# The order of wide and narrow matmuls in the up products of a two-layer decoder

## The chip, the cores and the metric

The kernel runs on one core of a Trainium2 chip. The metric is the time of one execution on the device, in microseconds. The engines are called as in the profile: PE (TensorE, with PEld for its weight loads), DVE (VectorE), ACT (ScalarE), POOL (GpSimd) and SP (SyncE, which here issues the transfers).

## The reference

The input has 256 tokens of 2048 channels. A first layer mixes tokens by an RWKV-7 recurrence (32 heads of 64) and then runs a multilayer perceptron (MLP); a second one runs attention over a window of 128 tokens, with shared keys and values, and then an MLP of its own. All arrays are float32. The change lies in the two MLPs:

```python
D_FF = 4 * D_MODEL          # 8192

def squared_relu_mlp(xn, w_up, w_down):
    return jnp.square(jax.nn.relu(xn @ w_up)) @ w_down

h = h + squared_relu_mlp(rms_norm(h, mlp_norm[layer]), mlp_w_up[layer], mlp_w_down[layer])
```

## The kernel before

**Products in high and low parts.** PE multiplies in a rounded form of float32 (fp32r). To keep the precision, each operand is split into a high part, which is the rounded value, and a low part, which is the rest, and a product is the sum high x high + high x low + low x high. Inputs are kept as tiles of 128 channels with both parts side by side: `xt[kt]` is 128 x (2 x 256 tokens). Weights come from memory in tiles `raw` of 128 x 1024 and are split in pieces of 512 columns: ACT writes the high part `wh` (L146), DVE the low part `wl` (L147). Each of the two has three buffers, `raw` has four.

**Up products.** `gemm_c` makes 128 of the 8192 hidden channels for all 256 tokens. The weights are the stationary operand, the inputs move. One piece of weights holds four blocks of 128 x 128, for four input tiles. Per block there are two matmuls: one of 512 moving columns, high weights with both parts of the input (L168), and one of 256, low weights with the high part alone (L170). Both add into one bank of PSUM: the left half collects high x high and low x high, the right half high x low. A product has four pieces, an MLP 64 products, and there are two MLPs.

**What follows.** ACT copies the right half, DVE adds the left one, applies the gain and the ReLU, ACT squares, and ACT and POOL split the result into high and low parts again (L1056 to L1062). After 16 up products come the down products of these 2048 hidden channels (`gemm_t`, L182 to L184): there the inputs are stationary and the weights move, always 512 columns.

**What sets the order.** In the RWKV part PE's order is the one written in the code (`rwkv_in_order`); short dependent products stand between pieces of long ones (`product`, L345 and L347, written like `gemm_c`). The rest is placed by a scheduler that simulates the engines and takes what is ready; where the code says `manual_schedule` for PE, the written order is kept among the matmuls inside, and others can still be placed between them. `gemm_t` uses it for its blocks, `gemm_c` does not. Each engine then runs its own list in order.

**Names in the prediction's steps.** `x_m` are the MLP's transposed inputs and `ps_u`, `ps_d` the sums of up and down products. In the RWKV part `merges` fetches blocks of inverses from memory as `X` and `XT`, 64 partitions at a time (L845), and multiplies them (L858); `three` (L686) makes the gate product with three matmuls of 256 columns for each of two blocks.

Of the kernel before, what the change touches and what calls it, by code (L numbers as in the profile page):

```python
# [17 lines left out]
P = 128  # L18
T = 256
D = 2048  # L20
KT = D // P
# [6 lines left out]
NXA, NXB = 32, 16  # L28
# pieces of long products between the short ones, in microseconds of the tensor engine
F1 = (5.0, 0.7, 3.0, 2.5, 3.0)  # L30
# [63 lines left out]

# columns of a pair's key side: [R | A | (B, K) | k' | E | XT]
S1W = 7 * T + 4
# [9 lines left out]
class K:  # L106
# [18 lines left out]

    # [P, 512] working tiles of the RWKV part, by role
    def t2(self, tag, name):
# [8 lines left out]

    # raw weights as four (hi, lo) pieces of 512 columns
    def split(self, raw, q, name):
# [19 lines left out]

    # out[c, t] (two halves: high x parts, low x parts) = sum_k W[k, c] x[k, t]
    def gemm_c(self, src, xt, name):  # L160
        nc = self.nc
        raw = self.load(src.rearrange("p k c -> p (k c)"), name)
        ps = self.acc(f"ps_{name}")
        for q in range(4):
            wh, wl = self.split(raw, q, f"{name}_{q}")
            for j in range(4):
                kt = 4 * q + j
                nc.tensor.matmul(ps, wh[:, j * P:(j + 1) * P], xt[kt].rearrange("p a t -> p (a t)"),  # L168
                                 start=(kt == 0), stop=False, skip_group_check=True)
                nc.tensor.matmul(ps[:, :T], wl[:, j * P:(j + 1) * P], xt[kt][:, 0, :],  # L170
                                 start=False, stop=(kt == KT - 1), skip_group_check=True)
        return ps

    # out[t, n] for one chunk of 512 columns, two token halves
    def gemm_t(self, srcs, xt, name, evac):
        nc = self.nc
        pss = [self.acc(f"ps_{name}_{t}") for t in range(2)]
        nk = 4 * len(srcs)

        def part(t, kb, wh, wl):  # L180
            tt = slice(t * P, (t + 1) * P)
            nc.tensor.matmul(pss[t], xt[kb][:, 0, tt], wh, start=(kb == 0), stop=False)  # L182
            nc.tensor.matmul(pss[t], xt[kb][:, 1, tt], wh, start=False, stop=False)  # L183
            nc.tensor.matmul(pss[t], xt[kb][:, 0, tt], wl, start=False, stop=(kb == nk - 1))  # L184
        todo = []
        for g, src in enumerate(srcs):
            raw = self.load(src.rearrange("p k c -> p (k c)"), f"{name}_{g}")
            for q in range(4):
                kb = 4 * g + q
                todo.append((kb, *self.split(raw, q, f"{name}_{g}_{q}")))  # L190
                # the last two blocks go by token half, so that the first half is done early
                if kb != nk - 2:
                    with self.tc.manual_schedule(engines={mybir.EngineType.PE}):
                        for t in range(2):
                            for w in todo:
                                part(t, *w)
                    todo = []
        for t in range(2):
            evac(t, pss[t])

    # 1/sqrt(v) for small v [P, n], v > 0
    def rsqrt(self, v, n, name):
# [3 lines left out]

    # rstd [P, 2] over the channels of h[t][n]
    def rstd(self, h, name, vector=False):
# [18 lines left out]

    # [P, T] tile whose column t holds rstd of token t
    def rstd_row(self, rs, name):
# [9 lines left out]

    # (h * gain)^T as high and low parts, one list of KT tiles per gain  # L240
    def xT(self, h, gains, name, tags, banks=("ps",)):
# [65 lines left out]

    # ---------------------------------------------------------------- RWKV
    # The tensor engine runs in the order written here: short dependent products, with pieces of long
    # products between them (fill) to cover the way through the other engines and back.  # L310
    def rwkv_in_order(self, h):
        with self.tc.manual_schedule(engines={mybir.EngineType.PE}):
            return self.rwkv()

    # run queued pieces for about us microseconds of the tensor engine
    def fill(self, us):
# [36 lines left out]
    def rwkv(self):  # L353
        tc, nc, d = self.tc, self.nc, self.d
        with ExitStack() as es:
# [5 lines left out]

            # scratch in DRAM: per pair results of the key side; block images of the inverses
            self.sp = [dr.tile([2, P, S1W - T], F32, name=f"sp{c}") for c in range(NPAIR // 2)]
            self.za = [dr.tile([64, 32, 64], F32, name=f"za{i}") for i in range(2)]
            self.zx = [dr.tile([4, 32, 32, 64], F32, name=f"zx{i}") for i in range(2)]
            # derived per-channel vectors
            hv = self.cp.tile([P, 4 * KT], F32, name="hv")
# [11 lines left out]

            # ---- norm, transpose, shift  # L380
            x = self.load_h0
# [4 lines left out]
            for g in range(KT // 2):  # L386
# [6 lines left out]
                ps = self.ps(f"xT{g}", banks[g])  # L393
                for jj in range(2):
                    kt = 2 * g + jj
# [27 lines left out]
            first = []  # L423
# [83 lines left out]

            # ---- key side: two pairs to a step; merges of the inverses follow three steps later
            xr, xv = [None] * KT, [None] * KT
# [9 lines left out]
            side = self.key_low(0)  # L519
# [6 lines left out]
            for s in range(8):  # L526
# [26 lines left out]
                if s < 7:  # L553
                    side = self.key_low(2 * s + 2)
# [8 lines left out]

            # ---- value side: one pair to a step
            stream = deque([(0, 2), (1, 2)] + [(p, i) for p in range(2, NPAIR) for i in (0, 2)])
            zs = []
            h = [[None] * 4 for _ in range(2)]
# [78 lines left out]
            for n in range(2):  # L646
                for t in range(2):
                    evac_n(n)(t, wo[n][t])
            # the first layer's rows are transposed between the last products
            self.xt0 = [[]]  # L650
# [12 lines left out]

    # the first block of columns of the output product, as far as zs goes
    def out_part(self, w, n, zs, out, bank):
# [16 lines left out]

    # out += w^T x, both as (high, low)
    def three(self, out, w, x, start, stop):
        for i, (a, b) in enumerate(((0, 0), (0, 1), (1, 0))):
            self.nc.tensor.matmul(out, w[a], x[b], start=(start and i == 0), stop=(stop and i == 2))  # L686

    # sum of the two halves of a channel-major product
    def join(self, dst, ps, name):
# [7 lines left out]

    # key side of pairs p, p + 1: decay and rate
    def key_low(self, p):
# [8 lines left out]
        for j in J:  # L708
            q = p + j
# [5 lines left out]
            nc.scalar.activation(ta[:, j], ps[:, T:], AF.Tanh, bias=self.hv[:, 16 + q:17 + q], scale=0.5)  # L715
        # decay: sums within a chunk, before and through each token
        nc.vector.tensor_scalar(pd[:, :, :, 1:], pd[:, :, :, 1:], 1.0, None, ALU.add)
# [7 lines left out]

    # sums of squares by token and head
    def key_norm(self, p, k, side):
# [32 lines left out]

    # normalised keys (negated), and what the chunks take from them
    def key_mid(self, p, k, side):
# [20 lines left out]

    # products within the chunks, masked
    def key_high(self, p, V, ats):
# [17 lines left out]

    # (I - Mab)^-1 for the four pairs of a group: 16 x 16 diagonal blocks by substitution, one block to a
    # partition
    def substitute(self, g):
# [19 lines left out]

    # blocks of the inverses of pairs 2c, 2c + 1 merged to 32, then to 64; X^T is kept
    def merges(self, c, ats):
# [22 lines left out]

        # out[po, :, :, n] = L[k, :, :, m]^T R[k, :, :, n]
        def mm(nm, po, k, L, m, R, n):
# [35 lines left out]

    # value side of pair p, before the chunks: scores, values by token, bonus  # L890
    def prep(self, p, rv, st):
# [6 lines left out]
        nc.vector.tensor_tensor(R, self.c4(r), E[:, :, 1:], ALU.mult)  # L898
        # scores, transposed: rows (b s | k s) for head 0, (k s | b s) for head 1; columns (r t | a t)
        SC = [[None] * NCH for _ in range(2)]  # L900
# [12 lines left out]
        yield 1.75  # L913
        # by token: (b, k) of each chunk; values under room for S (SV) and for the state products (ST)
        kr = [H[1], H[0]]
# [32 lines left out]

    # chunk by chunk
    def chain(self, p, st, hop):  # L950
# [46 lines left out]

    # group norm, by token
    def post(self, p, yps, ob):
# [15 lines left out]

    # back to channels; affine, bonus, gate
    def post_pe(self, p, post, zs):
# [23 lines left out]

    # ---------------------------------------------------------------- MLP
    def mlp(self, h, layer, xtag, htag):
# [25 lines left out]

    # ---------------------------------------------------------------- attention  # L1070
    def attention(self, h):
        tc, nc, d = self.tc, self.nc, self.d
        with ExitStack() as es:
# [7 lines left out]
            rs = self.rstd(h, "a")  # L1081
            # rotary tables with the norm gains folded in: [t][c * g | swapped signs]
            tabs = {}
# [29 lines left out]

            # shared keys and values
            vs = [ap.tile([P, T], F32, name=f"v_{t}") for t in range(2)]
# [71 lines left out]

    # transposed probabilities of heads a, a + 1: [key, (block 0: own | block 1: previous, own) x q]
    def softmax(self, a2, qT, kT, a, bank):
# [90 lines left out]
```

## Time and profile before

| | us |
|---|---|
| median of three timed runs | 2432.09 |
| the three runs | 2429.99, 2432.09, 2434.12 |
| span of the profiled execution | 2429.5 |
| PE busy in that span | 2342.7 |
| L168, 2048 matmuls of 512 columns, busy | 723.9 |
| L170, 2048 matmuls of 256 columns, busy | 574.9 |

The span goes from the first to the last instruction of the program in one profiled execution; the page states no other time of that execution. It lies 2.6 us below the median and 0.5 us below the fastest run. Busy time counts overlapping matmuls of a group once, and their ends are modelled, so a group's mean duration is longer than the step from one start to the next. A line "A <- B" in a list of waits says that A stood idle until B was done.

The run falls into four parts: RWKV until about 732 us, the first MLP until 1449, attention until about 1714, and the second MLP to the end. In each MLP four runs of up products take turns with four runs of down products.

### The profile page before, as it was taken

To read this page: it belongs to the slowest core of one execution; us is meant where nothing else is said; L and a number is where in the kernel's file an instruction comes from. 1 tells how busy PE (TensorE), PEld (TensorE's weight loads), DVE (VectorE), ACT (ScalarE), POOL (GpSimd) and SP (SyncE) were. 2 spreads that over 40 slices of the span, in tenths; PEclk is the share of its full clock that TensorE was granted. 3 is DMA by queue.
4 is the path that set the end of the run, shared out by engine and by line. 5 is a ranking of instruction groups with operands and counts; after the bars stand their busy time and mean duration, and the time that the engine had idled before them with its cause. 6 is when DMAs were issued, how large, how long until landed. Compare 5 with 4: busy or idle time off the path is not lost.

```text
span 2429.5 us, 40469 instructions
## 1 busy us (share of the span) xinstructions
PE 2342.7 (96%) x14448; PEld 1925.8 (79%) x14448; DVE 1560.0 (64%) x3126; ACT 1284.5 (53%) x2563; POOL 487.0 (20%) x635
## 2 busy tenths in 40 slices
PE   5878799999999999999999999999999999999999
PEld 4666677777788888888888887777888888888887
DVE  7887667777666656556556666766655655665655
ACT  5545333333356546546546565765654554554654
POOL 3657322334301101101001001641110110110100
PEclk9998899999999999999999999999999999999999
DMA  4665644444465565665565555334565655556565
GB/s 139 204 194 163 175 146 142 141 140 137 146 195 181 188 196 184 190 192 189 191 191 186 187 182 185 111 112 156 183 190 192 190 190 192 187 188 196 184 199 174
DMA packets 149642, 425.64 MB, mean 175 GB/s; under 512 B 38848, under 2 KB 46784, under 8 KB 149440
## 3 DMA queue, kind: packets, MB, share of 16 engines
q1 hardware_dynamic: 148000, 420.62, 54.5%
q10 hardware_dynamic: 1440, 2.44, 0.3%
q8 instruction: 113, 1.85, 0.3%
q14 instruction: 89, 0.73, 0.1%
HBM read 403.05 MB, written 19.96 MB: 174 GB/s over the span
## 4 chain that ended last, share of the span: by engine, by line
PE 88%; DVE 4%; DMA 4%; issue 1%; SPq 1%; ACT 1%; POOL 1%; ACTq 0%; DVEq 0%; POOLq 0%
PE ps_u L168 20%; PE ps_u L170 10%; PE ps_d L184 9%; PE ps_d L183 9%; PE ps_d L182 9%; PE ps_v L345 3%; PE ps_r L345 3%; PE ps_wo L678 2%; PE ps_wo L680 2%; PE ps_wo L679 2%; PE ps_q L184 1%; PE ps_q L182 1%; PE ps_q L183 1%; PE ps_v L347 1%; PE ps_r L347 1%
## 5 line engine op out<-in xcount | busy, mean ns | idle before, releaser
L168 PE MATMUL ps_u<-x_m,wh_u 128*128 128x512 f32 x2048 | 723.9, 399 | 0.0
L170 PE MATMUL ps_u<-x_m,wl_u 128*128 128x256 f32 x2048 | 574.9, 281 | 0.0
L147 DVE TENSOR_TENSOR wl_d<-raw_d,wh_d 128x512 fp32r<-128x512 f32 x512 | 354.5, 693 | 292.8 <-ACT wh_d L146 274.6
L147 DVE TENSOR_TENSOR wl_u<-raw_u,wh_u 128x512 fp32r<-128x512 f32 x512 | 354.8, 693 | 267.7 <-ACT wh_u L146 261.3
L146 ACT ACTIVATE wh_d<-raw_d 128x512 fp32r<-128x512 f32 x512 | 323.7, 632 | 347.2 <-DVE wl_d L147 260.6
L168 PEld LDWEIGHTS ps_u<-x_m,wh_u 128*128 128x128 f32 x2048 | 384.6, 188 | 95.1
L146 ACT ACTIVATE wh_u<-raw_u 128x512 fp32r<-128x512 f32 x512 | 324.2, 633 | 256.1 <-PE ps_u L168 238.3
L184 PE MATMUL ps_d<-wl_d,h 128*128 128x512 f32 x1024 | 399.0, 390 | 1.6 <-DVE wl_d L147 1.6
L182 PE MATMUL ps_d<-wh_d,h 128*128 128x512 f32 x1024 | 398.8, 389 | 0.0
L183 PE MATMUL ps_d<-wh_d,h 128*128 128x512 f32 x1024 | 398.5, 389 | 0.0
L170 PEld LDWEIGHTS ps_u<-x_m,wl_u 128*128 128x128 f32 x2048 | 386.9, 189 | 0.6
L1062 POOL TENSOR_TENSOR h<-w,h 128x256 fp32r<-128x256 f32 x128 | 115.6, 904 | 1124.7 <-ACT h L1061 1096.0
L184 PEld LDWEIGHTS ps_d<-wl_d,h 128*128 128x128 f32 x1024 | 192.2, 188 | 42.1 <-DVE wl_d L147 2.3
L182 PEld LDWEIGHTS ps_d<-wh_d,h 128*128 128x128 f32 x1024 | 192.2, 188 | 39.8
L183 PEld LDWEIGHTS ps_d<-wh_d,h 128*128 128x128 f32 x1024 | 192.2, 188 | 39.7
L345 PE MATMUL ps_k<-lk,wh_k 128*128 128x512 f32 x256 | 98.9, 423 | 6.9 <-DVE lk L414 6.3
L345 PE MATMUL ps_v<-lv,wh_v 128*128 128x512 f32 x256 | 101.7, 426 | 0.0
L345 PE MATMUL ps_r<-lr,wh_r 128*128 128x512 f32 x256 | 101.7, 427 | 0.0
L146 ACT ACTIVATE wh_v<-raw_v 128x512 fp32r<-128x512 f32 x64 | 40.4, 631 | 97.7 <-PE ps_v L345 37.4
L146 ACT ACTIVATE wh_r<-raw_r 128x512 fp32r<-128x512 f32 x64 | 40.3, 630 | 79.9 <-PE ps_v L345 32.9
L347 PE MATMUL ps_k<-lk,wl_k 128*128 128x256 f32 x256 | 75.6, 295 | 5.6 <-DVE wl_k L147 5.5
L1219 POOL TENSOR_SCALAR s<-s,den 128x128 f32<-128x128 f32 x64 | 61.8, 981 | 77.3 <-DVE den L1215 30.5
(308 smaller groups left out, 3754.9 us busy)
## 6 DMA issues: line engine op xcount, KB each, us to landing
raw_u<-in_up SPq DMA_DIRECT2D x256, 512.0 KB
raw_d<-in_down SPq DMA_DIRECT2D x256, 512.0 KB
raw_k<-in_wrkv SPq DMA_DIRECT2D x32, 512.0 KB
raw_r<-in_wrkv SPq DMA_DIRECT2D x32, 512.0 KB
raw_v<-in_wrkv SPq DMA_DIRECT2D x32, 512.0 KB
raw_wout<-in_wout SPq DMA_DIRECT2D x32, 512.0 KB
raw_q<-in_wq SPq DMA_DIRECT2D x32, 512.0 KB
S1b<-sp SPq DMA_DIRECT2D x16, 770.0 KB
```

Source lines behind the costliest of these rows:

```text
L146: nc.scalar.activation(wh, src, AF.Copy)
L147: nc.vector.tensor_tensor(wl, src, wh.bitcast(F32), ALU.subtract)
L168: nc.tensor.matmul(ps, wh[:, j * P:(j + 1) * P], xt[kt].rearrange("p a t -> p (a t)"), start=(kt == 0), stop=False, skip_group_check=True)
L170: nc.tensor.matmul(ps[:, :T], wl[:, j * P:(j + 1) * P], xt[kt][:, 0, :], start=False, stop=(kt == KT - 1), skip_group_check=True)
L182: nc.tensor.matmul(pss[t], xt[kb][:, 0, tt], wh, start=(kb == 0), stop=False)
L183: nc.tensor.matmul(pss[t], xt[kb][:, 1, tt], wh, start=False, stop=False)
L184: nc.tensor.matmul(pss[t], xt[kb][:, 0, tt], wl, start=False, stop=(kb == nk - 1))
L345: nc.tensor.matmul(ps, wh[:, j * P:(j + 1) * P], xt[kt].rearrange("p a t -> p (a t)"), start=(kt == 0), stop=False, skip_group_check=True)
L347: nc.tensor.matmul(ps[:, :T], wl[:, j * P:(j + 1) * P], xt[kt][:, 0, :], start=False, stop=(kt == KT - 1), skip_group_check=True)
L678: nc.tensor.matmul(pss[t], zs[kb][:, 0, tt], wh, start=(kb == 0), stop=False)
L1062: nc.gpsimd.tensor_tensor(hx[:, 1, :], w, hx[:, 0, :].bitcast(F32), ALU.subtract)
L1219: nc.gpsimd.tensor_scalar(ss[i][:, sl[t]], ss[i][:, sl[t]], den[:, i, t:t + 1], None, ALU.mult)
```

## The change

In `gemm_c` the four matmuls of 512 columns of a piece are issued first, then the four of 256, and both loops stand under `manual_schedule`, so that PE keeps this order. Everything else in the file differs in comments only. The core of the diff:

```diff
     def gemm_c(self, src, xt, name):
         nc = self.nc
         raw = self.load(src.rearrange("p k c -> p (k c)"), name)
         ps = self.acc(f"ps_{name}")
         for q in range(4):
             wh, wl = self.split(raw, q, f"{name}_{q}")
-            for j in range(4):
-                kt = 4 * q + j
-                nc.tensor.matmul(ps, wh[:, j * P:(j + 1) * P], xt[kt].rearrange("p a t -> p (a t)"),
-                                 start=(kt == 0), stop=False, skip_group_check=True)
-                nc.tensor.matmul(ps[:, :T], wl[:, j * P:(j + 1) * P], xt[kt][:, 0, :],
-                                 start=False, stop=(kt == KT - 1), skip_group_check=True)
+            with self.tc.manual_schedule(engines={mybir.EngineType.PE}):
+                for j in range(4):
+                    kt = 4 * q + j
+                    nc.tensor.matmul(ps, wh[:, j * P:(j + 1) * P], xt[kt].rearrange("p a t -> p (a t)"),
+                                     start=(kt == 0), stop=False, skip_group_check=True)
+                for j in range(4):
+                    kt = 4 * q + j
+                    nc.tensor.matmul(ps[:, :T], wl[:, j * P:(j + 1) * P], xt[kt][:, 0, :],
+                                     start=False, stop=(kt == KT - 1), skip_group_check=True)
         return ps
```

The lines of `gemm_c` are L169 and L173 afterwards, and lines behind it move by three.

PE's list in the middle of the first run of up products (product 9, first piece), before. `wh` and `wl` are the parts of the weights, the last field is the shape of the result:

```order
L168 MATMUL ps_u_9_9516<-x_m_0_8504,wh_u_9_0_9517 128x512
L170 MATMUL ps_u_9_9516<-x_m_0_8504,wl_u_9_0_9518 128x256
L168 MATMUL ps_u_9_9516<-x_m_1_8507,wh_u_9_0_9517 128x512
L170 MATMUL ps_u_9_9516<-x_m_1_8507,wl_u_9_0_9518 128x256
L168 MATMUL ps_u_9_9516<-x_m_2_8559,wh_u_9_0_9517 128x512
L170 MATMUL ps_u_9_9516<-x_m_2_8559,wl_u_9_0_9518 128x256
L168 MATMUL ps_u_9_9516<-x_m_3_8562,wh_u_9_0_9517 128x512
L170 MATMUL ps_u_9_9516<-x_m_3_8562,wl_u_9_0_9518 128x256
```

The same place afterwards:

```order
L169 MATMUL ps_u_9_9624<-x_m_0_8504,wh_u_9_0_9625 128x512
L169 MATMUL ps_u_9_9624<-x_m_1_8507,wh_u_9_0_9625 128x512
L169 MATMUL ps_u_9_9624<-x_m_2_8559,wh_u_9_0_9625 128x512
L169 MATMUL ps_u_9_9624<-x_m_3_8562,wh_u_9_0_9625 128x512
L173 MATMUL ps_u_9_9624<-x_m_0_8504,wl_u_9_0_9626 128x256
L173 MATMUL ps_u_9_9624<-x_m_1_8507,wl_u_9_0_9626 128x256
L173 MATMUL ps_u_9_9624<-x_m_2_8559,wl_u_9_0_9626 128x256
L173 MATMUL ps_u_9_9624<-x_m_3_8562,wl_u_9_0_9626 128x256
```

The same eight matmuls stand in groups by width; of eight changes of width per piece, counting the one to the next piece, two are left.

PE's list at the start of the first MLP, where the products 0 to 2 are mixed, before; `x_m_12` to `x_m_15` are the last inputs to be transposed:

```order
L168 MATMUL ps_u_1_9020<-x_m_12_8896,wh_u_1_3_9057 128x512
L168 MATMUL ps_u_0_8958<-x_m_15_8910,wh_u_0_3_8995 128x512
L170 MATMUL ps_u_0_8958<-x_m_15_8910,wl_u_0_3_8996 128x256
L170 MATMUL ps_u_1_9020<-x_m_12_8896,wl_u_1_3_9058 128x256
L168 MATMUL ps_u_1_9020<-x_m_13_8899,wh_u_1_3_9057 128x512
L170 MATMUL ps_u_1_9020<-x_m_13_8899,wl_u_1_3_9058 128x256
L168 MATMUL ps_u_1_9020<-x_m_14_8907,wh_u_1_3_9057 128x512
L170 MATMUL ps_u_1_9020<-x_m_14_8907,wl_u_1_3_9058 128x256
L168 MATMUL ps_u_1_9020<-x_m_15_8910,wh_u_1_3_9057 128x512
L170 MATMUL ps_u_1_9020<-x_m_15_8910,wl_u_1_3_9058 128x256
L168 MATMUL ps_u_2_9082<-x_m_0_8504,wh_u_2_0_9083 128x512
L170 MATMUL ps_u_2_9082<-x_m_0_8504,wl_u_2_0_9084 128x256
```

And afterwards, the stretch that ends with the first product's last piece:

```order
L169 MATMUL ps_u_1_9032<-x_m_12_8896,wh_u_1_3_9078 128x512
L169 MATMUL ps_u_1_9032<-x_m_13_8899,wh_u_1_3_9078 128x512
L169 MATMUL ps_u_1_9032<-x_m_14_8907,wh_u_1_3_9078 128x512
L169 MATMUL ps_u_2_9106<-x_m_0_8504,wh_u_2_0_9107 128x512
L169 MATMUL ps_u_2_9106<-x_m_1_8507,wh_u_2_0_9107 128x512
L169 MATMUL ps_u_2_9106<-x_m_2_8559,wh_u_2_0_9107 128x512
L169 MATMUL ps_u_2_9106<-x_m_3_8562,wh_u_2_0_9107 128x512
L169 MATMUL ps_u_0_8958<-x_m_15_8910,wh_u_0_3_9004 128x512
L173 MATMUL ps_u_0_8958<-x_m_12_8896,wl_u_0_3_9005 128x256
L173 MATMUL ps_u_0_8958<-x_m_13_8899,wl_u_0_3_9005 128x256
L173 MATMUL ps_u_0_8958<-x_m_14_8907,wl_u_0_3_9005 128x256
L173 MATMUL ps_u_0_8958<-x_m_15_8910,wl_u_0_3_9005 128x256
```

The four wide matmuls of product 2 now come ahead of the first product's matmul with `x_m_15`; before, product 2 came behind all of product 0 and 1.

The scheduler's choices change in a few places far from the up products too. SP's list in the RWKV part, where the blocks for the first two merges are fetched (`X_1933` and `XT_1934` for the first, the others for the second), before:

```order
L155 DMA raw_k_0_0_2053<-in_wrkv 128x1024
L155 DMA raw_k_2_0_2104<-in_wrkv 128x1024
L845 DMA X_1933<-zx_114 64x1x512
L845 DMA XT_1934<-zx_114 64x1x512 x2
L845 DMA X_2251<-zx_114 64x1x512
L845 DMA XT_2252<-zx_114 64x1x512
L845 DMA X_1933<-zx_114 64x1x512
L845 DMA X_2251<-zx_114 64x1x512
L845 DMA XT_2252<-zx_114 64x1x512
```

And afterwards:

```order
L155 DMA raw_k_0_0_2053<-in_wrkv 128x1024
L155 DMA raw_k_2_0_2104<-in_wrkv 128x1024
L848 DMA X_1933<-zx_114 64x1x512 x2
L848 DMA XT_1934<-zx_114 64x1x512 x2
L848 DMA X_2251<-zx_114 64x1x512 x2
L848 DMA XT_2252<-zx_114 64x1x512 x2
```

Both halves of the first `X` are now issued first; before, its second half was the sixth of the eight fetches.

## Rows read from the trace of the kernel before

**Rows 1.** The page: busy time and share by engine; granted clock in 40 slices.

```profile
PE 2342.7 (96%) x14448; PEld 1925.8 (79%) x14448; DVE 1560.0 (64%) x3126; ACT 1284.5 (53%) x2563; POOL 487.0 (20%) x635
...
PEclk9998899999999999999999999999999999999999
```

**Rows 2.** PE's waits, 749 us to the end: total us, times, longest.

```profile
PE ps_d L184 <- DVE wl_d L147: 1.6, 1, 1.6
PE ps_wo L678 <- ACT o L1162: 0.2, 1, 0.2
```

**Rows 3.** Sums by stretch, with the head of the view: an up run, a down run.

```profile
core 0: us, PE busy (x) PEld busy (x) DVE busy (x) ACT busy (x) POOL busy (x), PEclk, DMA share, GB/s
911.47:1001.91 90.44, 90.44 (x513) 78.47 (x512) 55.76 (x96) 55.44 (x109) 13.27 (x15) 1.00 0.60 186
1001.91:1088.98 87.07, 87.07 (x386) 72.08 (x385) 48.69 (x74) 41.48 (x68) 0.88 (x1) 1.00 0.60 194
```

**Rows 4.** Timeline at an up run's start: start us, us, engine, line, operation, tiles.

```profile
911.47 0.39 PE L168 MATMUL ps_u<-x_m,wh_u 128*128 128x512 f32 x1
911.48 0.19 PEld L170 LDWEIGHTS ps_u<-x_m,wl_u 128*128 128x128 f32 x1
911.70 0.28 PE L170 MATMUL ps_u<-x_m,wl_u 128*128 128x256 f32 x1
...
911.81 0.40 PE L168 MATMUL ps_u<-x_m,wh_u 128*128 128x512 f32 x1
```

**Rows 5.** Timeline, six matmuls of 256 columns (L686) behind a 512.

```profile
678.14 0.39 PE L680 MATMUL ps_wo<-wl_wout,z 128*128 128x512 f32 x1
...
678.37 0.40 PE L686 MATMUL yt<-sg,wh_g 128*128 128x256 f32 x2
678.49 0.19 PEld L686 LDWEIGHTS yt<-sg,wl_g 128*128 128x128 f32 x1
678.60 0.28 PE L686 MATMUL yt<-sg,wl_g 128*128 128x256 f32 x1
...
678.72 0.41 PE L686 MATMUL yt<-sg,wh_g 128*128 128x256 f32 x2
...
678.96 0.28 PE L686 MATMUL yt<-sg,wl_g 128*128 128x256 f32 x1
```

**Rows 6.** PE's timeline at the two MLPs' starts: groups of two pairs.

```profile
741.30 0.63 PE L168 MATMUL ps_u<-x_m,wh_u 128*128 128x512 f32 x2
741.76 0.40 PE L170 MATMUL ps_u<-x_m,wl_u 128*128 128x256 f32 x2
742.00 0.40 PE L168 MATMUL ps_u<-x_m,wh_u 128*128 128x512 f32 x1
...
1722.68 0.62 PE L168 MATMUL ps_u<-x_m,wh_u 128*128 128x512 f32 x2
...
1723.38 0.40 PE L168 MATMUL ps_u<-x_m,wh_u 128*128 128x512 f32 x1
```

**Rows 7.** Waits of the weights' split, 753 to 1449 us.

```profile
ACT wh_u L146 <- PE ps_u L168: 115.0, 230, 0.9
```

**Rows 8.** ScalarE's timeline at the first MLP's start.

```profile
740.91 0.47 ACT L260 ACTIVATE x_m<-xT_m,par 128x256 fp32r<-128x256 f32 x1
...
743.13 1.21 ACT L146 ACTIVATE wh_u<-raw_u 128x512 fp32r<-128x512 f32 x2 [0.62 <-PE ps_u L168]
```

**Rows 9.** Timeline, SyncE's issues for the merges and PE's wait.

```profile
169.12 0.65 SPq L845 DMA_DIRECT2D X<-zx  x1
...
172.08 1.07 SPq L845 DMA_DIRECT2D X<-zx  x2
...
182.50 0.80 PE L858 MATMUL p<-X,mk 64*64 64x64 f32 x10 [5.02 <-DMA X<-zx]
```

**Rows 10.** PE's waits, 0 to 760 us.

```profile
PE nb L769 <- ACT R L744: 14.4, 4, 6.5
```

**Rows 11.** Timeline, gate matmuls of 256 columns behind 64-column ones.

```profile
358.89 0.50 PE L686 MATMUL yt<-sg,wh_g 128*128 128x256 f32 x2
...
359.23 0.28 PE L686 MATMUL yt<-sg,wl_g 128*128 128x256 f32 x1
```

## The prediction

> **What bounds the kernel now.** I read the page's busy line first. TensorE (PE) is busy 96% of the span, VectorE 64%, ScalarE 53%, and the granted clock stands at its upper level (2.4 GHz, shown as 9 of 10 or more) in all but the first slices [rows 1]. Then the list of what PE waits for, from 749 us to the end, which covers nearly all of both MLPs and the attention between them: one wait of 1.6 us and one of 0.2 us in 1680 us [rows 2]. So in the part that the change touches PE never lacks anything; the time is how fast it gets through its own list. The sums by stretch give that rate: a full run of 16 up products (64 pieces of weights, 512 matmuls) takes 90.44 us, and a full run of down products (384 matmuls of 512 columns) takes 87.07 us, both with PE busy all the time at clock 1.00 [rows 3]. That is
>
> - 90.44 / 64 = 1.413 us for a piece now, 0.3533 us for a pair (one matmul of 512, one of 256 columns);
> - 87.07 / 384 = 0.2267 us for a matmul of 512 columns among its like.
>
> The "busy" and "mean ns" columns can't be used for this: a 512 shows as 0.40 us and a 256 as 0.28, but the next one starts long before that. What counts is start to start: 911.47, 911.70, 911.81 in the timeline [rows 4]. The load of the next weights (PEld) starts 0.01 us after the matmul before it, so it lies behind that matmul.
>
> **What the change does to PE.** It adds no matmul, no load and no byte. It changes which width follows which: now 512, 256, 512, 256, ...; afterwards four 512, four 256. Three kinds of spacing must be priced.
>
> 512 after 512: 0.2267 us, from the down run.
>
> 256 after 256: the gate product of the RWKV part issues six matmuls of 256 columns with 128 x 128 weights in a row. They start at 678.37 (two), 678.60, 678.72 (two) and 678.96: five spacings in 0.59 us, 0.118 us each, with loads in between that are recorded as 0.19 us long and so overlap each other [rows 5]. The 512 ahead of them lasts 0.23 us (678.14 to 678.37), so the step from wide to narrow costs nothing unusual there.
>
> By these two a pair would be 0.2267 + 0.118 = 0.3447 us, but alternating it takes 0.3533: 8.6 ns more. If that excess belongs to the switching, three of four switches go.
>
> A piece in the new order stands nowhere in the trace, but its small sister does. Where the start of each MLP mixes two accumulators, the order 512, 512, 256, 256 occurs, four times in all. The first goes from 741.30 to 742.00, the last from 1722.68 to 1723.38: 0.70 us for two pairs, with both switches in it [rows 6], against 2 x 0.3533 = 0.707. To make a whole piece of it I add two 512 and two 256 among their like:
>
> 0.700 + 2 x 0.2267 + 2 x 0.118 = 1.389 us, which is 0.024 us less than 1.413.
>
> There are 2 layers x 64 products x 4 pieces = 512 pieces: 512 x 0.0237 = **12.1 us less**. The bounds: with no cost of switching at all a piece is 4 x 0.2267 + 4 x 0.118 = 1.379, which gives 17.6 us; if every further pair is no better than those in the groups of two, it is 2 x 0.700 = 1.400, which gives 6.7 us. I take the middle because it alone uses a row for each kind of spacing.
>
> **What else moves.** ScalarE and VectorE, which split the weights into high and low parts, keep their order apart from the starts of the MLPs. Each is busy some 56 of the 90.44 us of an up run [rows 3]; a run of 88.9 us (64 x 1.389) leaves them 37% idle. In the 700 us of the first MLP ScalarE waited 115 us in 230 waits for PE to give a high part's buffer back [rows 7]. That cover grows: the four 512s end three 256s, some 0.35 us, earlier than now, and the low part is first needed 4 x 0.2267 = 0.91 us after the high part rather than 0.23 us. Cost nothing; the weights' transfers (DMA share 0.60 in the run) would have to be 1.7% quicker, also nothing.
>
> At the start of each MLP PE's list is mixed differently: the four 512s of the third product now stand ahead of the last transposed input of the first. ScalarE is the tight engine there: it works on the last transposed input at 740.91 and first waits for PE again before 743.13 [rows 8]. In the new list the four need a high part that ScalarE makes after that input. Between 0 and 1.5 us per layer; I take 0.25, since PE has other products queued for most of that time: 0.5 us more.
>
> One thing moves far from the change. On SyncE the fetches of the first block inverses change order. Now the second half of the first X is the sixth of eight, issued at 172.08; PE stops 5.02 us for an X, until 182.50 [rows 9]. Afterwards it is second, about where 169.8 stands now, 2.3 us sooner. The landing can move by that, or by the whole 5.02 us if the transfers queued ahead are what delays it, or not at all. What follows on PE waits four times, 14.4 us in all, for a ScalarE result of the key side [rows 10], which can swallow the gain. Bounds 4.5 us less to 1 us more; I take 1.0 us less.
>
> **Sum.** -12.1 + 0.5 - 1.0 = -12.6 us. On the profiled execution's span, 2429.5 us, that is 2416.9. The median of the three timed runs is 2.6 us above that span, and the gain does not depend on this: 2432.1 - 12.6 = **2419.5 us**.
>
> **Rivals.**
>
> *No change (0.10).* The 8.6 ns are not a price of switching but belong to products whose weights are stationary and whose inputs move, as against the down and gate products. For it: the groups of two save 7 ns at most, though half of the switches are gone. Against: 512 and 256 run at the same steady rate in several kinds of product, and the groups do come out below two pairs. A piece stays at 1.413 and the time is 2432.1 + 0.5 - 1.0 = 2431.6. The Trainium skill, "TensorE: Matmul & The Clock Gate", section "Back-to-back issue gap", has a rule to the same effect: start to start is a matmul's columns over the clock plus some 2.5 ns, so the order would not matter at all. By that rule an estimate for a piece is 4 x 215.8 + 4 x 109.2 = 1300 ns in either order; the trace has 1413, so something else than columns counts here, and the measurement decides.
>
> *The supply becomes the limit (0.04).* PE passes through the up products faster than the split refills, and at the eight passages from up to down it waits as once now, 1.6 us for a low part [rows 2]: 8 x 1.6 = 12.8 us, and the gain is gone: 2419.5 + 12.8 = 2432.3. Against it: the idle share above.
>
> *Slower (0.06).* A load that follows matmuls of another shape may not be hidden. At 358.89 the same six gate matmuls come behind small 64-column ones, and the third starts at 359.23 instead of 0.24 us after the first: 0.34 us, some 0.10 us more [rows 11]. If a run of four 512s leaves the array so that the first load of the 256s pays this once per piece, it is 512 x 0.10 = 51 us: 2419.5 + 51 = 2471. It decides the sign from 24 ns per piece, a quarter of that price. Against it: in [rows 5] the same matmuls come behind 512s and the price is not paid.
>
> **How the numbers follow.** The forecast case has 0.80. Its own range is made of the bounds: 2432.1 - 17.6 - 4.5 = 2410 and 2432.1 - 6.7 + 1.0 + 3.0 = 2429.4. The end of the range, 2432, takes in half of the two cases of no gain, which leaves out somewhat under 0.2. A measurement of this kernel can tell about 0.2% from no change, here 4.9 us: faster means below 2427.2. Of the forecast case some 0.02 lies between that and 2429.4; so 0.78 faster, 0.16 same (0.02 and the two cases of no gain), 0.06 slower.
>
> **What would show it.** In the profile of the changed kernel a full up run should take 88.9 us instead of 90.44 (88.2 to 89.6 by the bounds), down runs 87.07 as now, with PE's waits in the MLPs still under 3 us in all. The timeline of a piece should show spacings of 0.227 between 512s and 0.118 between 256s. The wait for X should end some 2 us earlier, with part of that lost again at the next waits. The forecast is wrong if the 512s of a piece stand 0.235 us apart, if one spacing at the seam between 512s and 256s is above 0.3 us, or if low parts are waited for.

## The result, and the profile after

| | us |
|---|---|
| before, median of four runs | 2432.43 (2429.99 to 2434.12) |
| changed, median of four runs | 2418.77 (2417.71 to 2419.26) |
| ratio | 0.9944, 95% interval 0.9932 to 0.9956 |
| span of the profiled execution | 2416.4, before 2429.5 |

The total is 0.7 us from the forecast. Its parts are not: the profile gives the up products 5.2 us where 12.1 were forecast, and the RWKV part 7.7 us where 1.0 was. The sum came out by two errors that cancel.

The page of the changed kernel, the lines that answer to [rows 1]:

```profile
PE 2337.0 (97%) x14448; PEld 1925.1 (80%) x14448; DVE 1558.5 (64%) x3126; ACT 1283.8 (53%) x2563; POOL 483.0 (20%) x635
...
PEclk9999899999999999999999999999999999999999
```

PE is as full as before. Each slice is some 60.7 us; the clock's digit for the fourth one (182 to 243 us before), where the RWKV part changed, was 8 and is 9 now. The sums of an up and a down run, as in [rows 3], and of a stretch of the RWKV part that is read below:

```profile
903.25:993.03 89.78, 89.78 (x513) 78.47 (x512) 55.49 (x96) 55.67 (x110) 13.37 (x15) 1.00 0.56 188
993.03:1080.12 87.09, 87.09 (x386) 72.08 (x385) 48.89 (x73) 41.20 (x68) 0.74 (x1) 1.00 0.57 193
178.00:191.50 13.50, 12.19 (x185) 10.50 (x181) 11.52 (x31) 7.46 (x16) 6.09 (x8) 1.00 0.71 201
```

An up run takes 89.79 us (89.78 by the rounded ends of the window) against 90.44: 0.65 us less, eight times 5.2 us. A piece is 89.79 / 64 = 1.403 us, not the 1.389 of the forecast and outside its bounds for a run (88.2 to 89.6). Down runs are the same. The timeline of a piece, which merges matmuls of one line into one row:

```profile
921.47 1.09 PE L169 MATMUL ps_u<-x_m,wh_u 128*128 128x512 f32 x4
922.40 0.63 PE L173 MATMUL ps_u<-x_m,wl_u 128*128 128x256 f32 x4
922.87 1.09 PE L169 MATMUL ps_u<-x_m,wh_u 128*128 128x512 f32 x4
```

Start to start, the four 512s take 0.93 us, 0.2325 each, and the four 256s 0.47, 0.1175 each. The narrow ones are as forecast. The wide ones are not: among their like in the down products they take 0.2267.

In the RWKV part, SyncE's fetches and PE's first use of X, against [rows 9]:

```profile
168.71 1.24 SPq L848 DMA_DIRECT2D X<-zx  x2
...
177.92 1.10 PE L861 MATMUL p<-X,mk 64*64 64x64 f32 x32
```

Both halves of X are issued together, and the 32 matmuls start at 177.92 with no idle time ahead of them; before, PE stopped for 5.02 us and started again at 182.50. What came after that wait in the kernel before, in the view of sums:

```profile
182.50:199.80 17.30, 17.30 (x180) 15.73 (x181) 10.07 (x21) 6.76 (x15) 8.34 (x10) 0.63 0.36 110
```

After the 5 us of idle the mean granted clock was 0.63 for 17.3 us: a good part of it at the lower of the two levels (1.2 GHz). The changed kernel does nearly the same work (185 matmuls for 180) in 13.5 us at 1.00, of which 1.3 us are idle. At this place, then, the wait had cost its own length and some 4 us of slow clock behind it. Over the whole part ahead of the first up product this does not add up so. The sums of that part, before and after:

```profile
0.00:732.76 732.76, 652.04 (x5882) 516.23 (x5882) 533.25 (x1274) 322.90 (x682) 284.99 (x430) 0.97 0.51 160
0.00:725.08 725.08, 651.28 (x5881) 515.17 (x5882) 532.19 (x1274) 323.08 (x682) 282.03 (x430) 0.97 0.51 162
```

PE's busy time falls by 0.8 us only, its idle time by 6.9 (80.7 to 73.8), and the mean clock is 0.97 in both: the changed kernel has slow stretches elsewhere, such as 160 to 178 us at 0.81, where the kernel before had 0.90 from 160 to 182.5. So the first up product starts at 725.1 us against 732.8 almost wholly because PE waits less. 5.0 us of that is the wait for X; a later wait, for XT, is 3.8 us shorter, and other waits give part back. That wait before:

```profile
PE x L858 <- DMA XT<-zx: 7.0, 2, 5.9
```

PE's waits after the change, in the two lists that answer to [rows 2] and [rows 10]:

```profile
PE ps_d L187 <- DVE wl_d L147: 1.2, 1, 1.2
...
PE nb L772 <- ACT R L747: 14.5, 4, 4.8
...
PE x L861 <- DMA XT<-zx: 3.2, 2, 2.0
```

In the MLPs nothing new is waited for. By parts of the span: RWKV -7.7; eight up runs -5.2; the mixing at the two starts +0.3; the one wait for a low part -0.4. That is -13.0, and the spans differ by 13.1.

### The profile page after: what moved, and what is told of

Its sections match the earlier page's. It is cut to its first block, busy times and chain, and to the rows that moved or that the text cites. A ratio compares the mean times of both kernels' runs of the same rounds, so it can differ in the third digit from the quotient of the medians.

```text
span 2416.4 us, 40472 instructions
## 1 busy us (share of the span) xinstructions
PE 2337.0 (97%) x14448; PEld 1925.1 (80%) x14448; DVE 1558.5 (64%) x3126; ACT 1283.8 (53%) x2563; POOL 483.0 (20%) x635
## 5 line engine op out<-in xcount | busy, mean ns | idle before, releaser
L169 PE MATMUL ps_u<-x_m,wh_u 128*128 128x512 f32 x2048 | 559.1, 394 | 0.0
L169 PEld LDWEIGHTS ps_u<-x_m,wh_u 128*128 128x128 f32 x2048 | 350.6, 189 | 47.6 <-ACT wh_u L146 0.2
L173 PEld LDWEIGHTS ps_u<-x_m,wl_u 128*128 128x128 f32 x2048 | 313.8, 189 | 43.1
L173 PE MATMUL ps_u<-x_m,wl_u 128*128 128x256 f32 x2048 | 325.7, 281 | 0.0
```

## The experiments

**The two parts of the change, each alone.** The change orders the matmuls and it puts them under `manual_schedule`. Only the second (the code here and below is shortened, against the changed kernel):

```diff
     for j in range(4):
         matmul(ps, wh[j], xt[kt])             # 512 columns
-    for j in range(4):
         matmul(ps[:, :T], wl[j], xt[kt][:, 0]) # 256 columns, under the same manual_schedule
```

> Only the second part of the change: 512 and 256 alternate as before, but the piece stands under manual_schedule. PE's list is then word for word that of before; on SyncE the fetches of the first X and XT stand in the order of the changed kernel. Theory: the first 732 us lose 7.7 us by that order alone (725 at the first up product), an up run stays at 90.44 us, and the time is 2432.4 - 7.7 = 2424.7. Rival (the early gain came from the grouping, or differs from execution to execution): first up product at 732.8, time 2432.4.

Measured: 2425.07 us against 2431.38 for before on the same chip, ratio 0.9972 (0.9961 to 0.9984). In the sums and in the timeline of its profile:

```profile
903.34:993.78 90.44, 90.44 (x514) 78.43 (x512) 55.78 (x96) 55.46 (x109) 13.29 (x15) 1.00 0.59 186
```

```profile
177.10 1.10 PE L859 MATMUL p<-X,mk 64*64 64x64 f32 x32
```

The up run is that of before to the last digit; the wait for X is gone, and the first up product starts at 724.6. PE's list is identical to that of before. VectorE's and ScalarE's lists have one exchange of neighbours each; all else that differs is SyncE's order. So a scope that does not reorder a single matmul makes the kernel 6.3 us faster (3.9 to 9.5 by the interval), through the scheduler's choice of DMA order 550 us earlier in the program.

Only the first part:

```diff
-    with self.tc.manual_schedule(engines={mybir.EngineType.PE}):
+    if True:
         for j in range(4): ...   # four 512
         for j in range(4): ...   # four 256
```

> Only the first part of the change: four 512 then four 256, without manual_schedule. PE's list is that of the changed kernel, SyncE's that of before. Theory: the wait of 5.0 us for X at 182.5 is back and the first up product starts at 732.8; an up run takes 89.79 us; time 2432.4 - 5.4 = 2427.0. Rival (the order on SyncE has no part in the time): 2418.8, as the changed kernel.

Measured: 2425.61 us, ratio 0.9978 (0.9969 to 0.9987). The sums, and the timeline:

```profile
909.65:999.44 89.79, 89.79 (x513) 78.47 (x512) 55.53 (x96) 55.73 (x110) 13.39 (x15) 1.00 0.60 188
```

```profile
181.19 1.12 PE L861 MATMUL p<-X,mk 64*64 64x64 f32 x16 [4.92 <-DMA X<-zx]
```

The up run is the changed kernel's, and the wait of 4.9 us for X is back, with SyncE's old order; the first up product starts at 731.5. It is 6.9 us behind that of the other run, and here too most is idle time of PE: 5.4 us (70.1 against 64.7), with 1.5 us of busy time. The two ratios multiply to 0.9950, within the interval of the whole change. The rivals of both runs fall: neither is the early gain due to the grouping, nor is SyncE's order without effect.

**Why a 512 takes 0.2325 us in a piece.** The up products have stationary weights and moving inputs, the down products the reverse. The first suspicion was that what moves decides.

```diff
-    matmul(ps, wh[:, j*P:(j+1)*P], xt[kt])
+    st = (xt[kt][:, 0, :P], wh[:, j*P:(j+1)*P])[layer]
+    mv = (xt[kt], wh)[layer]
+    matmul(ps, st, mv)
```

> The changed kernel, but the 512s multiply other data of the same shape: in the first MLP an input tile stands for the weights as well (stationary x, moving x), in the second the piece of weights stands for the inputs as well (stationary w, moving w). In the changed kernel (stationary w, moving x) 512 after 512 takes 0.234 us, in the down products (stationary x, moving w) 0.227. Theory: what moves decides; the first MLP shows 0.234, the second 0.227. Rival one, what is stationary decides: 0.227 in the first, 0.234 in the second. Rival two, neither does, but the 256s in the neighbourhood: 0.234 in both.

Measured in one execution. First MLP (inputs on both sides; its list has two groups of wide ones in a row here and there), then second MLP (weights on both sides):

```profile
905.97 2.00 PE L171 MATMUL ps_u<-x_m 128*128 128x512 f32 x8
907.81 0.40 PE L174 MATMUL ps_u<-x_m,wl_u 128*128 128x256 f32 x2
...
1900.52 1.09 PE L171 MATMUL ps_u<-wh_u 128*128 128x512 f32 x4
1901.45 0.63 PE L174 MATMUL ps_u<-x_m,wl_u 128*128 128x256 f32 x4
```

Eight 512s in 1.84 us (0.230), four in 0.93 (0.2325). Over all of them, 512 after 512 takes 0.2325 us in the first MLP and 0.2335 in the second. Neither comes near 0.227: the theory and its first rival fall, the 256s in the neighbourhood remain.

```diff
     for a, wx in enumerate((wh, wl)):
         for j in range(4):
+            if layer == 0: matmul(ps, wx[j], xt[kt])          # 8 x 512 per piece
+            else: 256 columns at a time, wh twice and wl once  # 12 x 256 per piece
```

> The changed kernel with one width only in the up products: in the first MLP the low weights too go over 512 columns (8 matmuls of 512 per piece; this adds low x low), in the second the 512s are cut in two (12 matmuls of 256 per piece). Theory (what moves decides): 0.234 per 512, an up run of 64 x 8 x 0.234 = 119.8 us; 0.118 per 256, an up run of 64 x 12 x 0.118 = 90.6 us. Rival (mixing widths costs): 0.2267 per 512, 116.1 us in the first MLP, and the same 90.6 in the second.

Measured in one execution; the sums of an up run in the first and in the second MLP:

```profile
933.42:1049.48 116.06, 116.06 (x514) 96.10 (x512) 56.88 (x96) 59.42 (x110) 11.16 (x15) 1.00 0.46 147
1991.28:2083.43 92.15, 92.15 (x769) 92.15 (x768) 56.14 (x96) 55.61 (x110) 13.76 (x15) 1.00 0.59 185
```

116.06 / 512 = 0.2267 us per 512, with the inputs moving; 92.15 / 768 = 0.120 per 256. The rival holds for the 512s: alone they run at the down products' rate, and mixing widths costs. The 90.6 us that both had for the 256s is missed: in a long row of them one takes 0.120, not the 0.118 of the five spacings in [rows 5]. A piece free of that cost would take 4 x 0.2267 + 4 x 0.120 = 1.387 us. Alternating costs 26 ns over this, groups of four 16 ns. The premise of the prediction, that the excess belongs to mixing, was right; that four in a row remove three quarters of it was not.

**How the cost depends on the group.** Longer groups (16 is one whole product):

```diff
+    G = (8, 16)[layer]
+    for g in groups of G input tiles:
+        for kt in g: matmul of 512
+        for kt in g: matmul of 256
```

> The changed kernel with longer groups: eight 512 then eight 256 in the first MLP, sixteen and sixteen (a whole product) in the second. Measured so far per piece: 1.413 us alternating, 1.403 in fours, and 4 x 0.2267 + 4 x 0.120 = 1.387 if each width ran as in the kernel of one width. Theory: each step from one width to the other costs about 8 ns (16 ns for the two of a piece in fours); eights give 1.395 us per piece and an up run of 89.3 us, sixteens 1.391 and 89.0. Rival: any 512 in a product of mixed widths is slower, however the group is cut; 89.8 us in both. Risk: sixteens could make PE wait for a low part, since all four of a product are needed close together with three buffers.

Measured in one execution: 2419.57 us. The scheduler mixed the groups of neighbouring products, so that in both MLPs PE's list has fours and eights; the sixteens were thus not tried. What the list has is telling, first MLP:

```profile
920.07 1.09 PE L166 MATMUL ps_u<-x_m,wh_u 128*128 128x512 f32 x4
921.00 1.12 PE L171 MATMUL ps_u<-x_m,wl_u 128*128 128x256 f32 x8
921.96 2.00 PE L166 MATMUL ps_u<-x_m,wh_u 128*128 128x512 f32 x8
923.80 0.64 PE L171 MATMUL ps_u<-x_m,wl_u 128*128 128x256 f32 x4
924.27 1.09 PE L166 MATMUL ps_u<-x_m,wh_u 128*128 128x512 f32 x4
```

Four 512s behind 256s take 0.93 us here too. Eight take 1.84, so their second half takes 0.91, 0.2275 each: the rate recovers only after some four of them. Eight 256s take 0.96 (0.120), four 0.47 (0.1175): these start a little fast. Eight and eight make two pieces in 2.80 us, 1.400 each. Neither the theory nor the rival has this shape; the price is that of a slow start behind a change to wide, partly given back by a quick start behind a change to narrow.

```diff
+    G = (2, 4)[layer]
+    low = ps if layer == 0 else another PSUM bank
     ...
-    matmul(ps[:, :T], wl[j], ...)
+    matmul(low[:, :T], wl[j], ...)
```

> First MLP: groups of two 512 and two 256. Second MLP: groups of four as in the changed kernel, but the 256s add into a PSUM bank of their own that nobody reads (low x high is left out of the result). Theory (a price of 8 ns per change of width): groups of two have four changes per piece, 1.387 + 0.033 = 1.420 us, an up run of 90.9 us, which would be more than alternating; the bank changes nothing, 89.8 us. Rival (the price belongs to the same sums being written again in another width): groups of two between 1.403 and 1.413, 89.8 to 90.4 us, and with a bank of their own the second MLP's runs fall to 64 x 1.387 = 88.8 us.

Measured in one execution; the sums of an up run in groups of two, and the timeline of the second MLP with its own bank (`lo_u`):

```profile
903.87:993.03 89.16, 89.16 (x513) 77.80 (x512) 55.56 (x96) 55.53 (x110) 13.30 (x15) 1.00 0.60 189
```

```profile
1900.89 2.02 PE L168 MATMUL ps_u<-x_m,wh_u 128*128 128x512 f32 x8
1902.75 0.52 PE L173 MATMUL lo_u<-x_m,wl_u 128*128 128x256 f32 x3
```

Groups of two are the best of those tried: 89.16 us, 1.393 per piece, only 6 ns over the sum of single widths, with twice as many changes of width as fours. That is below the theory's 90.9 and below the rival's 89.8 to 90.4: a fixed price per change is refuted, and grouping more does not always save more. With a bank of its own for the 256s, eight 512s take 1.86 us, not less than 1.84; an up run and a down run together, 1795.59 to 1972.36, take 176.77 us, in the changed kernel 903.25 to 1080.12, 176.87. The bank isn't the cause either. In groups of two a 512 takes 0.233 on the mean and a 256 only 0.115: the slow start is paid, but nearly balanced by the quick one.

**The version that this points to.** Groups of two in both MLPs, `G = 2`, and the changed kernel beside it on the same chip:

> Groups of two 512 and two 256 in both MLPs, under manual_schedule, otherwise the changed kernel. In the first MLP of the run before, an up run took 89.16 us in groups of two, 0.63 us less than in fours. Theory (the sizes of the groups add up as measured there): eight up runs, 8 x 0.63 = 5.0 us less than the changed kernel, 2413.7 us if that one takes 2418.7. Rival (the second MLP, or the starts of the MLPs, give it back): 2418 to 2419, as the changed kernel.

> The changed kernel itself once more, on the same chip and beside the same runs of before as the kernel with groups of two: 2418.8 us and a ratio of 0.9944.

Measured, five runs each: groups of two 2415.21 us (2412.90 to 2415.72), ratio 0.9930 (0.9917 to 0.9942); the changed kernel 2420.18 (2414.11 to 2422.89), ratio 0.9952 (0.9939 to 0.9966). The sums of a run in each MLP with groups of two:

```profile
902.76:991.93 89.17, 89.17 (x514) 77.81 (x513) 55.50 (x96) 55.43 (x110) 13.32 (x15) 1.00 0.59 189
1878.12:1967.29 89.17, 89.17 (x514) 77.81 (x513) 55.51 (x96) 55.33 (x110) 13.75 (x15) 1.00 0.59 189
```

In the traces the gain over the changed kernel is plain: some 0.6 us in each of the eight runs, 5 us in all. In the times the medians differ by 5.0 us as expected, but the two intervals touch: the changed kernel's runs spread over 9 us. The traces show where such a spread can come from. Up and down runs repeat to a few hundredths of a microsecond; the first up product starts anywhere from 722.1 to 728.8 us in eight profiles of kernels with SyncE's new order (722.1 and 725.1 are the same kernel), and at 731.5 and 732.8 in the two with the old one.

## Why the prediction was right, and where it was not

- *What bounds the kernel.* Right. PE's own rate was the time in both MLPs, and no wait took its place.
- *256 after 256, 0.118 us.* Right for a piece: 0.1175. In a long row it is 0.120, so the sum without any cost of mixing is 1.387 us, not the 1.379 of the bound.
- *512 after 512, 0.2267 us.* This is the step that failed: "To make a whole piece of it I add two 512 and two 256 among their like". In a piece no 512 is among its like. Behind 256s the first four run at 0.2325, and a piece has only four. The sign of being wrong that the prediction named, 0.235, was nearly reached. The group of two itself was read rightly from [rows 6]: 0.70 us in the trace of before, 89.16 / 128 = 0.697 in a full run. What was wrong is that rows of longer runs may be added to it. A pair takes 0.3533 us in alternation and 0.348 in twos; fours were extrapolated to 0.347 and came to 0.351. So the rate of a width among its like can't be added to a row from a mix.
- *The gain of the grouping.* 5.2 us against 12.1, below the lower bound of 6.7. That bound assumed that further pairs are no better than those in the groups of two; they are worse: 1.403 - 0.697 = 0.706 us for two of them.
- *The order on SyncE.* The mechanism was right, the place too, the size was not: 7.7 us in this pair of profiles, 6.3 by the times of the run with that order alone, against 1.0 and a bound of 4.5. What was mis-sized is the wait for X: the whole of it went, not half. The other large piece of the 7.7, the shorter wait for XT, is not shown to come from the order: with SyncE's old order and the grouping alone that wait is 2.1 us, less than in the changed kernel. The slow clock behind the wait for X was not counted either, but little of the gain can be put to it, since PE's busy time fell by 0.8 us. The fear that later waits would swallow the gain proved small: the waits for the key side's result are 14.5 us in all, as before.
- *The start of the MLPs, +0.5 us.* Sign and size were about right: +0.3 for both.
- *The rivals.* "No change" had its condition refuted: with the inputs moving and a single width, 512s run at 0.2267. Its observation, that the groups of two save little, was too low: in a full run they save 10 ns per two pairs, not 7 at most, and that is 20 of the 26 ns that mixing costs per piece. The rule of the Trainium skill named there ("TensorE: Matmul & The Clock Gate", "Back-to-back issue gap") is the page's formula for a matmul by itself, without regard to its neighbours, and it does not hold in these streams: the same eight matmuls take 1.413, 1.403 or 1.393 us by their order alone. "Slower" needed a load exposed at the seam; the seam costs nothing of the kind, since the four 256s behind 512s take 0.47 us. No low part is waited for beyond the one wait that was there.

So the sign and the total were right, and the total was lucky.

What stays open is why a 512 behind 256s is slow for some four matmuls. The runs exclude the kind of operand on either side and the PSUM bank; a fixed price per change of width does not fit. Groups of sixteen and other widths were not tried, nor was the rival that suggests itself: every matmul here has a weight load of its own, recorded as 0.19 us long, while 256s start every 0.12 us [rows 5], so the first 512s behind them might meet loads that are late. No run changes the loads alone. That VectorE's and ScalarE's one exchange each has no part in the early gain is argued from the trace, where the wait that vanishes is for X; it was not tried apart.

## What to carry to other kernels

Price a new order of matmuls by a stretch of the trace that has that very order, and don't extend it by rows from runs of another mix; if there is none, a single execution with one pattern per layer gives several rates at once. A scheduling scope or any other edit can reorder DMAs far away, so compare the lists of all engines. A slow clock behind a wait is worth counting, but check PE's busy and idle time over the whole part before a gain is put to it. When a forecast hits, compare its parts too.

## What was not expected of the hardware

- The order of the same eight matmuls (four of 512 columns, four of 256, float32 in its rounded form) changes their time by 1.4%: 1.413 us alternating, 1.403 in fours, 1.393 in twos, all at clock 1.00 and without a wait. One width alone runs at 0.2267 us per 512 and 0.120 per 256; an estimate from these two is 0.417 ns per column and 13 ns per matmul besides.
- Behind 256s, 512s take 0.2325 us for the first four and 0.2275 for the next four; behind 512s, 256s take 0.1175 for the first four, 0.120 over eight.
- 5.0 us without work on PE were followed by 17.3 us at a mean granted clock of 0.63, on work that took 12.2 us of busy time at 1.00 when the wait was gone. Over the whole RWKV part, though, PE's busy time was 652.0 us with the wait and 651.3 without.
